# One level of Strassen's algorithm for the first feed-forward product, and the second product in three slabs

## The chip, the cores and the metric

The kernel runs on one core of a Trainium2 chip. The metric is the device time of one execution in microseconds (us); 3 runs of the kernel before gave a median of 3263.25 us (3255.14 to 3263.57).

## What is computed

Two transformer layers with adaptive norms, then one block of a second kind, all on 512 tokens of width 1024 in float32. The change touches the feed-forwards, of which there are six: two in each of the two layers, two in the last block. Cut to what matters:

```
D_MODEL, SEQ, D_FF, DEPTH = 1024, 512, 2816, 2

def swiglu(h, w13, w2):
    a, b = jnp.split(h @ w13, 2, axis=-1)
    return (jax.nn.silu(a) * b) @ w2

cond = jax.nn.silu(c)
for l in range(DEPTH):
    mod = (cond @ ada_w[l] + ada_b[l]).reshape(B, N_SUBLAYERS, 3, 1, D)
    h = adaln_pre(x, norm_g[l, 0], mod[:, 0, 0], mod[:, 0, 1])
    x = x + 0.5 * mod[:, 0, 2] * swiglu(h, ffn1_w13[l], ffn1_w2[l])
    h = adaln_pre(x, norm_g[l, 1], mod[:, 1, 0], mod[:, 1, 1])
    ...
    x = x + mod[:, 1, 2] * (y @ w_out[l])
    h = adaln_pre(x, norm_g[l, 2], mod[:, 2, 0], mod[:, 2, 1])
    x = x + 0.5 * mod[:, 2, 2] * swiglu(h, ffn2_w13[l], ffn2_w2[l])
```

adaln_pre is a row norm times (1 + scale) plus shift. The last block has the same kind of feed-forward with separate gate and up weights, a row norm ahead of it and one behind it.

## The kernel before

Activations lie transposed: the 1024 features as 8 blocks (KD) of 128 partitions, the 512 tokens as columns. Every float32 matmul operand is split in two reduced-precision parts, hi and lo, and a product of two such pairs is three matmuls (`mm3`, lines 306 to 315): hi x hi, hi x lo, lo x hi, all with the weights as the stationary 128 x 128 operand. The normed rows lie in `hh` and `hl`.

A weight tile comes in by `wchunk` (line 287): one DMA of 512 KB on SP's queue into one of four `raw` buffers, then for each half an ACT copy `hi` (line 296) and a DVE subtraction `lo` (line 297).

`ffn` (line 668) is the feed-forward. Its first product goes over NF = 22 column chunks j of 128: `products(j)` loads the gate chunk and the up chunk and runs for each 8 blocks k x 3 matmuls of 512 columns into one PSUM bank. The chunk before is finished meanwhile: ACT takes silu of the gate, DVE multiplies by up, POOL makes the pair `uh`, `ul` (lines 717 and 720); in the last block DVE multiplies both by the row norm first (713, 714). All 22 chunks of `uh` and `ul` stay in SBUF. The second product goes over the 8 output blocks d: 22 x 3 matmuls of 512 columns into one bank, then `emit_d` adds to `x` and collects squares for the next norm. The last d is run in two halves of 256 tokens, and `link` (line 639) uses that: while PE runs the second half, DVE, ACT and POOL norm the first half of the tokens (`prenorm` or `scaled`), and the next item's first products start on that half (`first`, `first_k`).

The modulation vectors `mod` come from a background generator (`mod_steps`, line 377): a step loads one 512 KB tile of `ada_w` into a `raw` buffer and adds it, scaled, to `acc` on DVE (lines 384, 386); after eight steps PE transposes and DVE reduces. Each call of `bg` (line 499) makes a step three times in four; `mod(l, s, r)` runs the generator on where a vector that is needed is not there:

```
    def mod(l, s, r):
        while (l, s, r) not in mods:
            next(bg_it)
        return mods[l, s, r]
```

`bg` is called after each gate or up chunk from j = 1 on and after each third of a d in the second product. The program is written in this order, and a scheduler of the framework then sets the order of each engine's instructions, within what buffers and data allow; on the chip every engine takes its own in that order.

## Time and profile before

| | us |
|---|---|
| median of 3 runs | 3263.25 |
| profiled execution | 3260.46 |
| its span, first to last instruction | 3258.7 |
| PE busy | 3184.6 (98%) |
| DVE busy | 1725.5 (53%) |
| ACT busy | 1211.0 (37%) |
| POOL busy | 744.1 (23%) |

The mean granted clock of PE is 0.990 of full speed. A busy share is an average over stages: a feed-forward's stages are found by the names of their tiles (`hh` and `hl` against `uh` and `ul`), and the wait that counts in one is the wait of PE. PE is matmuls, PEld the weight loads that overlap them.

### The profile page before, as it was taken

The numbers are of one execution on the slowest core, as the hardware profiler recorded it, in microseconds if no ns is written. First come the engines' busy times: TensorE is split into PE (matmuls) and PEld (weight loads), VectorE is DVE, ScalarE is ACT, GpSimd is POOL, SyncE is SP. The second block draws the span as 40 slices with busy tenths as digits, with TensorE's granted clock in tenths as the row PEclk, the third lists the DMA queues.
The fourth block names the chain that finished last, engine by engine and source line by source line (L and its number), as shares of the span: only waits on it lengthen the run. The fifth ranks groups of instructions, "written<-read, shape, count | busy, mean of one in ns | idle before, by whom it ended". The sixth has DMA issues, their size and how long they took to land.

```text
span 3258.7 us, 43061 instructions
## 1 busy us (share of the span) xinstructions
PE 3184.6 (98%) x16168; PEld 2676.0 (82%) x16168; DVE 1725.5 (53%) x2942; ACT 1211.0 (37%) x2287; POOL 744.1 (23%) x754
## 2 busy tenths in 40 slices
PE   7999999999999999999999999999999999999998
PEld 5888887888888888888888888888888888888887
DVE  6555576666555555536766633344443444664433
ACT  3222254553222232224555532233223355652232
POOL 3221222214221222212122322211221210231111
PEclk8999999999999999999999999999999999999999
DMA  6555642113555445543321234333323355442233
GB/s 232 186 165 169 193 136 78 40 60 132 164 172 164 155 149 168 165 124 119 106 63 37 104 103 137 120 117 104 128 101 95 125 179 146 132 135 97 96 93 105
DMA packets 135825, 414.98 MB, mean 127 GB/s; under 512 B 16777, under 2 KB 30221, under 8 KB 135345
## 3 DMA queue, kind: packets, MB, share of 16 engines
q1 hardware_dynamic: 129408, 391.27, 37.2%
q0 software_dynamic: 6064, 20.76, 2.1%
q8 instruction: 127, 2.08, 0.3%
q14 instruction: 82, 0.66, 0.1%
q10 hardware_dynamic: 144, 0.21, 0.0%
HBM read 379.58 MB, written 22.51 MB: 123 GB/s over the span
## 4 chain that ended last, share of the span: by engine, by line
PE 90%; DVE 4%; ACT 2%; POOL 2%; issue 1%; DMA 1%; SPq 0%; DVEq 0%; ACTq 0%; POOLq 0%
PE m L311 14%; PE m L312 14%; PE m L308 14%; PE a L308 11%; PE a L312 11%; PE a L311 11%; PE o L1408 2%; PE pt L1402 1%; DVE lo L297 1%; PE a L1176 1%; PE a L1192 1%; PE num L1354 1%; DVE t L621 0%; DVE hl L623 0%; PE hid L947 0%
## 5 line engine op out<-in xcount | busy, mean ns | idle before, releaser
L297 DVE TENSOR_TENSOR lo<-raw,hi 128x512 fp32r<-128x512 f32 (+2 forms) x1056 | 805.6, 768 | 942.9 <-ACT hi L296 916.4
L296 ACT CAST hi<-raw 128x512 fp32r<-128x512 f32 (+2 forms) x1056 | 639.2, 611 | 1637.3 <-PE m L311 891.5
L308 PE MATMUL m<-hh,hi 128*128 128x512 f32 (+1 forms) x1728 | 669.4, 387 | 13.6 <-ACT hh L474 7.4
L311 PE MATMUL m<-hl,hi 128*128 128x512 f32 (+1 forms) x1728 | 663.7, 384 | 5.3 <-DVE hl L633 2.2
L312 PE MATMUL m<-hh,lo 128*128 128x512 f32 (+1 forms) x1728 | 661.2, 383 | 1.6 <-DVE lo L297 1.6
L311 PE MATMUL a<-hl,hi 128*128 128x512 f32 (+1 forms) x1264 | 476.3, 377 | 1.0 <-DVE hl L623 1.0
L308 PE MATMUL a<-hh,hi 128*128 128x512 f32 (+1 forms) x1264 | 475.9, 376 | 0.0
L312 PE MATMUL a<-hh,lo 128*128 128x512 f32 (+1 forms) x1264 | 475.3, 376 | 0.0
L308 PEld LDWEIGHTS m<-hh,hi 128*128 128x128 f32 x1728 | 327.9, 190 | 76.8 <-ACT hh L474 7.6
L311 PEld LDWEIGHTS m<-hl,hi 128*128 128x128 f32 x1728 | 328.2, 190 | 67.3 <-DVE hl L633 3.7
L312 PEld LDWEIGHTS m<-hh,lo 128*128 128x128 f32 x1728 | 327.6, 190 | 64.8 <-DVE lo L297 6.3
L717 POOL TENSOR_SCALAR uh<-u 128x512 fp32r<-128x512 f32 x132 | 112.3, 851 | 1101.7 <-DVE u L710 692.8
L311 PEld LDWEIGHTS a<-hl,hi 128*128 128x128 f32 x1264 | 239.4, 189 | 44.5 <-DVE hl L623 1.8
L312 PEld LDWEIGHTS a<-hh,lo 128*128 128x128 f32 x1264 | 239.3, 189 | 43.9 <-DVE lo L297 1.1
L308 PEld LDWEIGHTS a<-hh,hi 128*128 128x128 f32 x1264 | 239.3, 189 | 42.9 <-ACT hi L296 0.5
L308 PE MATMUL a<-uh,hi 128*128 128x512 f32 (+1 forms) x660 | 229.7, 348 | 0.6
L311 PE MATMUL a<-ul,hi 128*128 128x512 f32 (+1 forms) x660 | 229.5, 348 | 0.0
L312 PE MATMUL a<-uh,lo 128*128 128x512 f32 (+1 forms) x660 | 228.7, 347 | 0.0
L308 PE MATMUL m<-uh,hi 128*128 128x512 f32 x528 | 205.8, 390 | 0.0
L720 POOL TENSOR_TENSOR ul<-u,uh 128x512 fp32r<-128x512 f32 x132 | 203.0, 1538 | 10.8
L312 PE MATMUL m<-uh,lo 128*128 128x512 f32 x528 | 205.4, 389 | 0.0
L311 PE MATMUL m<-ul,hi 128*128 128x512 f32 x528 | 205.4, 389 | 0.0
(462 smaller groups left out, 3965.6 us busy)
## 6 DMA issues: line engine op xcount, KB each, us to landing
raw<-in_ada_dram SPq DMA_DIRECT2D x144, 512.0 KB, 4.3
raw<-in_f1a_dram SPq DMA_DIRECT2D x88, 512.0 KB, 4.2
raw<-in_f2a_dram SPq DMA_DIRECT2D x88, 512.0 KB, 3.6
raw<-in_win_dram SPq DMA_DIRECT2D x48, 512.0 KB, 3.3
raw<-in_g1a_dram SPq DMA_DIRECT2D x44, 512.0 KB, 3.6
raw<-in_g2a_dram SPq DMA_DIRECT2D x44, 512.0 KB, 3.6
raw<-in_f1b_dram SPq DMA_DIRECT2D x32, 512.0 KB, 3.7
raw<-in_f2b_dram SPq DMA_DIRECT2D x32, 512.0 KB, 3.5
```

The lines of the kernel that those rows point to most:

```text
L296: order["hi"] = S.copy(h, raw[:, s])
L297: order["lo"] = V.tensor_tensor(l, raw[:, s], h.bitcast(F32), op=ALU.subtract)
L308: i = PE.matmul(o, wh, xh, start=start, stop=False)
L311: PE.matmul(o, wh, xl, start=False, stop=False)
L312: j = PE.matmul(o, wl, xh, start=False, stop=stop)
L717: G.tensor_scalar(uh[:, j], u, 1.0, 0.0, op0=ALU.mult, op1=ALU.add)
L720: order["ul"] = G.tensor_tensor(ul[:, j], u, uh[:, j].bitcast(F32), op=ALU.subtract)
L1176: PE.matmul(p[:, bs_], B[:, bs_], Z[:, bs_], start=True, stop=True)
L1192: PE.matmul(p[:, bs_], RT[:, bs_], w[:, bs_], start=True, stop=True)
L1354: PE.matmul(pn[:, i * 65:i * 65 + 65], wt[j][:, (i - j) * 128:(i - j) * 128 + 128], vd[:, j, h], start=j == 0, stop=j == i)
L1402: PE.transpose(pt[:, j * 128:j * 128 + 128], t[:, j * 128:j * 128 + 128], ident)
L1408: PE.matmul(o, r[:, j * 128:j * 128 + 128], v, start=j == 0, stop=j == len(vs) - 1)
```

## The change

The first product. Features are split in two halves (k 0 to 3, 4 to 7), tokens in two (0 to 255, 256 to 511), and the output in gate and up: a 2 x 2 x 2 block product, which one level of Strassen's algorithm (in Winograd's form) does in seven products instead of eight. Each product p of chunk n is 4 blocks x 3 matmuls of 256 columns. The class `Units` lists the products in order (p = 1, 2, 5, 6, then 4 of the chunk before, 3, 7) together with the second product's pieces, and `ahead` prepares each one's weights up to five units early: sums of weights on POOL and DVE, then `hi` and `lo` as before. `product` runs a product, several of them accumulating in bank A, which ACT copies out in between (`snap`); `after` builds gate and up from the copies.

The tokens. `block0` prepares the first half of the tokens as before, and keeps the plain rows in `hk`; `block1` makes the differences of the halves and their pairs (second half of `hh`, `hl`, and the new `eh`, `el`). `mod_first` does the same at the start, with seven load buffers instead of fourteen.

The second product runs in three slabs of 6, 8 and 8 chunks, after chunk 6, chunk 14 and chunk 21; the first two are added into `x` by `emit_d.acc`. Only the slab's `uh` and `ul` are kept. `bg` is called once per chunk and after two in three pieces of a slab. The bias rows `rows` move to the mixer and to POOL's queue, and the post norm's factor `gh` moves from the copy out of PSUM to the norm.

The core of the diff:

```diff
...
     def x_open():
...
+        xbox["eh"] = p.tile([128, 4, 3, 256], F32R, name=nm("eh"))
+        xbox["el"] = p.tile([128, 4, 3, 256], F32R, name=nm("el"))
+        xbox["hk"] = p.tile([128, KD, 256], F32, name=nm("hk"))
...
-                        raw = IN.tile([128, 1024], F32, tag="raw", bufs=14, name=nm("raw"))
+                        raw = IN.tile([128, 1024], F32, tag="raw", bufs=7, name=nm("raw"))
...
             def norm(k):
-                t = w_("t")
+                f = dict(scale=m[1][:, k:k + 1], bias=m[0][:, k:k + 1])
+                t = two(hk[:, 2 * k:2 * k + 2]) if k < 4 else w_("t")
                 vec(V.tensor_scalar(t, xr[:, k], m[1][:, k:k + 1], m[0][:, k:k + 1], op0=ALU.mult, op1=ALU.add))
+                if k < 4:
+                    dep(S.activation(hh[:, k, HV[0]], xr[:, k, HV[0]], AF.Identity, **f), order["hi"])
+                    vec(V.tensor_tensor(t1[k], t[:, HV[1]], t[:, HV[0]], op=ALU.subtract))
+                    S.copy(hh[:, k, HV[1]], t1[k])
+                    vec(V.tensor_tensor(hl[:, k, HV[0]], t[:, HV[0]], hh[:, k, HV[0]].bitcast(F32), op=ALU.subtract))
+                    vec(V.tensor_tensor(hl[:, k, HV[1]], t1[k], hh[:, k, HV[1]].bitcast(F32), op=ALU.subtract))
+                    return
...
+                t2 = IN.tile([128, 3, 256], F32, tag="t2", bufs=2, name=nm("t2"))
+                vec(V.tensor_tensor(t2[:, 0], t[:, HV[1]], t1[k], op=ALU.subtract))
+                G.tensor_tensor(t2[:, 1], t[:, HV[1]], hk[:, 2 * k + 1], op=ALU.subtract)
+                G.tensor_tensor(t2[:, 2], t[:, HV[0]], t2[:, 0], op=ALU.subtract)
+                S.copy(eh[:, k], t2)
+                vec(V.tensor_tensor(el[:, k], t2, eh[:, k].bitcast(F32), op=ALU.subtract))
...
+    def hl_of(dst, src, n=None):
+        h, l = (a if n is None else a[n] for a in dst)
+        run["cur"].append(S.copy(h, src))
+        V.tensor_tensor(l, src, h.bitcast(F32), op=ALU.subtract)
+
+    def block0(k, make, shift):
+        t = xbox["hk"][:, k]
+        make(t, k, HV[0])
+        h, l = hh[:, k, HV[0]], hl[:, k, HV[0]]
...
+            run["cur"].append(S.activation(h, t, AF.Identity, bias=shift[:, k:k + 1]))
+            V.scalar_tensor_tensor(l, t, shift[:, k:k + 1], h.bitcast(F32), op0=ALU.add, op1=ALU.subtract)
...
+    def block1(tt, shift):
...
+        for k in range(4):
+            q1.append(tmp("q1"))
+            sub(q1[k][:, h0], tt[k][:, h0], hk[:, k])
+            hl_of((hh[:, k, h1], hl[:, k, h1]), q1[k][:, h0])
+        for k in range(4):
+            sub(q1[k][:, h1], tt[k][:, h1], q1[k][:, h0], sh(k))
+            hl_of((eh[:, k, 0], el[:, k, 0]), q1[k][:, h1])
...
+        for k in range(4):
+            q2.append(tmp("q2"))
+            sub(q2[k][:, h0], tt[k][:, h1], tt[k][:, h0], None if shift is None else ds[:, k:k + 1])
+            sub(q2[k][:, h1], hk[:, k + 4], q1[k][:, h1], sh(k))
+            v = q2[k].rearrange("p (a b) -> p a b", a=2)
+            hl_of((eh[:, k, 1:3], el[:, k, 1:3]), v)
...
+    NU, NA = 18, 3
+    SLABS = (list(range(16, 22)), list(range(0, 8)), list(range(8, 16)))
+    JS = sum(SLABS, [])
+
+    class Units:
...
+            for n in range(n0, len(JS)):
+                u += P_(n, 1, 2, 5, 6) + P_(n - 1, 4) + P_(n, 3, 7)
+                if n in ends:
+                    u += self.down(ends[n])
+            u += P_(len(JS) - 1, 4) + self.down(2)
...
+        def load(self, i):
+            self.live = [r for r in self.live if self.last[r] >= i]
+            while self.loads and len(self.live) < 4 and self.first[self.loads[0]] < i + 10:
...
+        def ahead(self):
...
+                if p == 5:
+                    new(G, 1, half(b, 0), half(b, 1), ALU.add)
+                elif p == 6:
+                    new(V, 2, S_[1], half(a, 0), ALU.subtract)
+                elif p == 3:
+                    new(G, 4, half(a, 1), S_[2], ALU.subtract)
+                    new(G, 3, half(a, 0), half(b, 0), ALU.subtract)
...
+            h, l = self.tile(fp, "hi")[:, :w], self.tile(fp, "lo")[:, :w]
+            order["hi"] = S.copy(h, src)
+            order["lo"] = V.tensor_tensor(l, src, h.bitcast(F32), op=ALU.subtract)
+            self.q.append((h, l))
...
+        def take(self):
+            while len(self.q) < 5 and self.at < len(self.units) and (box.get("fp") or not self.q):
+                self.ahead()
...
+        def product(self):
...
+                for i, (w, x) in enumerate(((wh, xh), (wh, xl), (wl, xh))):
+                    PE.matmul(q, w[:, s], x, start=p in (1, 2, 5) and k + i == 0, stop=k == 3 and i == 2,
+                              skip_group_check=p not in (1, 2, 5))
+            return n, p
+
+        def after(self, n, p, done, norm):
...
+            def snap(q, b):
+                S_[q] = fp.tile([128, 256], F32, tag="sn", bufs=5, name=nm("sn"))
+                S.copy(S_[q], S_[b][:, 0:256])
+            if p == 1:
+                snap(1, "A")
+            elif p == 2:
+                S_["g"] = fp.tile([128, 512], F32, tag="ga", bufs=3, name=nm("ga"))
+                V.tensor_tensor(S_["g"][:, HV[0]], S_[1], S_["B"][:, 0:256], op=ALU.add)
+            elif p == 5:
+                snap(5, "D")
+            elif p == 6:
+                snap(2, "A")
+            elif p == 3:
+                g = S_["g"]
+                V.tensor_tensor(g[:, HV[1]], S_[2], S_["D"][:, 0:256], op=ALU.add)
+                if norm is not None:
+                    V.tensor_tensor(g, g, box["r"], op=ALU.mult)
+                act(g, g, AF.Silu)
+                if norm is not None:
+                    V.tensor_tensor(g, g, box["r"], op=ALU.mult)
+            elif p == 7:
+                snap(3, "A")
+                S_["c"] = fp.tile([128, 256], F32, tag="c", bufs=2, name=nm("c"))
+                G.tensor_tensor(S_["c"], S_[3], S_[5], op=ALU.add)
+            else:
+                u, g = w_("u"), S_["g"]
+                V.tensor_tensor(u[:, HV[0]], g[:, HV[0]], S_["A"][:, 0:256], op=ALU.mult)
+                V.tensor_tensor(u[:, HV[1]], g[:, HV[1]], S_["c"], op=ALU.mult)
+                uh, ul = (fp.tile([128, 512], F32R, tag="u", bufs=NU, name=nm("u")) for _ in range(2))
+                S.copy(uh, u)
+                order["ul"] = G.tensor_tensor(ul, u, uh.bitcast(F32), op=ALU.subtract)
...
+                f.after(n, p, u, norm)
+                if p == 4:
+                    if n > 2 and side is not None:
+                        next(side, None)
                     bg()
...
+                for d in range(KD if s < 2 else KD - 2):
+                    q = psa() if d % 2 else psm()
+                    for h in range(2):
+                        x, ws = f.take()
+                        assert x == ("D", s, d, h)
+                        mm(q, ws, us[h * m:h * m + m], ALL, h * m, 2 * m)
+                        if (2 * d + h) % 3:
+                            bg()
+                    if s < 2:
+                        emit_d.acc(d, q, s == 0)
+                    else:
+                        emit_d(d, q, ALL, False)
...
+        def acc(d, q, first):
+            xd = xbox["x"][:, d]
+            V.scalar_tensor_tensor(xd, q, g()[:, d:d + 1], xd, op0=ALU.mult, op1=ALU.add)
...
```

How it moves instructions, at three places.

DVE at the link from the first mixer to the second feed-forward, before (`t` is the scaled row block, `hl` its low part with the shift `mod_2915`, `lo` a weight split, line 790 adds the old product to `x`):

```order
L790 SCALAR_TENSOR_TENSOR x_6512<-a_6762,mod_2116,x_6512 128x256
L621 SCALAR_TENSOR_TENSOR t_6903<-x_6512,mod_2541,r_6589 128x256
L621 SCALAR_TENSOR_TENSOR t_6907<-x_6512,mod_2541,r_6589 128x256
L297 TENSOR_TENSOR lo_6892<-raw_6889,hi_6891 128x512
L623 SCALAR_TENSOR_TENSOR hl<-t_6903,mod_2915,hh 128x256
L623 SCALAR_TENSOR_TENSOR hl<-t_6907,mod_2915,hh 128x256
```

and now (`hk` in place of `t`, `mod_8548` the same shift, `acc_8523` its sum, `ds` a difference of shifts):

```order
L711 SCALAR_TENSOR_TENSOR hk_8138<-x_8135,mod_4590,r_8215 128x256 x5
...
L895 TENSOR_TENSOR lo_8634<-raw_8507,hi_8633 128x512
L895 TENSOR_TENSOR lo_8646<-raw_8509,hi_8645 128x512
L386 TENSOR_SCALAR acc_8523<-raw_8524,cond 128x1024
L388 SCALAR_TENSOR_TENSOR acc_8523<-raw_8527,cond,acc_8523 128x1024
...
L388 SCALAR_TENSOR_TENSOR acc_8523<-raw_8545,cond,acc_8523 128x1024
L397 TENSOR_REDUCE mod_8548<-a_8549 128x4
L397 TENSOR_REDUCE mod_8548<-a_8555 128x4
L398 TENSOR_TENSOR mod_8548<-mod_8548,cols 128x8
L674 TENSOR_TENSOR ds_8750<-mod_8548 128x4
L663 SCALAR_TENSOR_TENSOR hl<-hk_8138,mod_8548,hh 128x256 x8
L895 TENSOR_TENSOR lo_8652<-S_8649,hi_8651 128x512
```

Between the scaled rows and their low parts there now stand the eight steps of a modulation vector and its reductions; before, that vector's steps stood inside the first feed-forward.

SP's DMA issues at the same link, now (`raw_8505` to `raw_8511` are the first weights of the second feed-forward, the `in_ada` loads belong to the eight steps; in the built program the first of these and all behind it have the address of `raw_8505`):

```order
L848 DMA raw_8505<-in_f2a_dram 128x1024
L848 DMA raw_8507<-in_f2a_dram 128x1024
L848 DMA raw_8509<-in_f2a_dram 128x1024
L848 DMA raw_8511<-in_f2a_dram 128x1024
L384 DMA raw_8524<-in_ada_dram 128x1024
L384 DMA raw_8527<-in_ada_dram 128x1024
...
L384 DMA raw_8545<-in_ada_dram 128x1024
L848 DMA raw_8808<-in_f2a_dram 128x1024
```

The weights take all four `raw` buffers ahead of the eight loads, and the next weights stand behind these.

DVE over one chunk in the middle of a first product, now (`S` a sum of weights, `ga` the gate, `sn` a copy out of PSUM, `A`, `B`, `D` the banks, `c` a sum on POOL):

```order
L895 TENSOR_TENSOR lo_3402<-raw_3132,hi_3401 128x512
L895 TENSOR_TENSOR lo_3427<-S_3422,hi_3426 128x512
L960 TENSOR_TENSOR u_3500<-ga_3292,c_3399 128x256
L895 TENSOR_TENSOR lo_3446<-S_3424,hi_3445 128x512
L940 TENSOR_TENSOR ga_3443<-sn_3418,B_3430 128x256
L895 TENSOR_TENSOR lo_3467<-raw_3313,hi_3466 128x512
L881 TENSOR_TENSOR S_3527<-S_3507,raw_3313 128x512
L895 TENSOR_TENSOR lo_3485<-raw_3313,hi_3484 128x512
L895 TENSOR_TENSOR lo_3510<-S_3507,hi_3509 128x512
L959 TENSOR_TENSOR u_3500<-ga_3292,A_3254 128x256
L895 TENSOR_TENSOR lo_3530<-S_3527,hi_3529 128x512
L947 TENSOR_TENSOR ga_3443<-sn_3482,D_3449 128x256
```

A chunk had four `lo` and one multiplication here; it has seven `lo`, one sum and four operations of 256 columns.

## Rows read from the trace of the kernel before

**Rows 1.** The page: its first line, busy time of each engine, the chain that ended last.

```profile
span 3258.7 us, 43061 instructions
...
PE 3184.6 (98%) x16168; PEld 2676.0 (82%) x16168; DVE 1725.5 (53%) x2942; ACT 1211.0 (37%) x2287; POOL 744.1 (23%) x754
...
PE 90%; DVE 4%; ACT 2%; POOL 2%; issue 1%; DMA 1%; SPq 0%; DVEq 0%; ACTq 0%; POOLq 0%
```

**Rows 2.** Timeline of PE: start us, duration us, instruction; 512 columns, then 256.

```profile
238.92 0.39 PE L308 MATMUL m<-hh,hi 128*128 128x512 f32 x1
...
243.00 0.39 PE L308 MATMUL m<-hh,hi 128*128 128x512 f32 x1
...
413.77 0.28 PE L312 MATMUL a<-uh,lo 128*128 128x256 f32 x1
...
417.73 0.28 PE L312 MATMUL a<-uh,lo 128*128 128x256 f32 x1
```

**Rows 3.** Groups of DVE: line, form, count | busy us, mean ns | idle before, releaser.

```profile
L623 DVE SCALAR_TENSOR_TENSOR hl<-t,mod,hh 128x256 fp32r<-128x256 f32 x80 | 37.6, 513 | 2.4 <-ACT hh L622 2.4
...
L1180 DVE TENSOR_TENSOR w<-a,lvl 128x256 f32<-128x256 f32 x56 | 22.7, 421 | 13.4 <-PE a L1176 13.1
...
L790 DVE SCALAR_TENSOR_TENSOR x<-a,mod,x 128x256 f32<-128x256 f32 x12 | 5.8, 479 | 27.8 <-PE a L312 27.8
...
L476 DVE TENSOR_TENSOR hl<-t,hh 128x512 fp32r<-128x512 f32 x8 | 6.4, 806 | 1.1 <-ACT hh L474 0.6
...
L473 DVE TENSOR_SCALAR t<-xr,mod,mod 128x512 f32<-128x512 f32 x8 | 5.3, 665 | 0.2
```

**Rows 4.** One line's instructions, L386 on DVE: ns min/median/max, first and last start.

```profile
L386 DVE SCALAR_TENSOR_TENSOR acc<-raw,cond,acc x112: 1271/1281/2319, 63.6 to 1388.4; 128x1024 f32<-128x1024 f32 x112
```

**Rows 5.** Groups of ACT and of POOL, columns as in rows 3.

```profile
L296 ACT CAST hi<-raw 128x512 fp32r<-128x512 f32 x944 | 582.1, 622 | 1464.6 <-PE m L311 804.7 <-PE a L311 593.9 <-PE a L1653 23.3
...
L720 POOL TENSOR_TENSOR ul<-u,uh 128x512 fp32r<-128x512 f32 x132 | 203.0, 1538 | 10.8
...
L619 POOL TENSOR_TENSOR t<-t,r 128x256 f32<-128x256 f32 x30 | 25.3, 845 | 34.6 <-ACT r L259 32.9
```

**Rows 6.** Timelines of DVE and of POOL, 325 to 330 us, columns as in rows 2.

```profile
325.00 0.68 DVE L297 TENSOR_TENSOR lo<-raw,hi 128x512 fp32r<-128x512 f32 x1
325.60 2.06 DVE L386 SCALAR_TENSOR_TENSOR acc<-raw,cond,acc 128x1024 f32<-128x1024 f32 x1
327.59 1.64 DVE L297 TENSOR_TENSOR lo<-raw,hi 128x384 fp32r<-128x384 f32 x1
...
325.17 1.42 POOL L580 TENSOR_TENSOR sq<-x 128x512 f32<-128x512 f32 x1 [13.54 <-DVE x L790]
326.66 2.15 POOL L588 TENSOR_TENSOR st<-st,sq 128x512 f32<-128x512 f32 x1
```

**Rows 7.** The same timelines near 1850 us.

```profile
1849.81 0.48 DVE L790 SCALAR_TENSOR_TENSOR x<-m,mod,x 128x256 f32<-128x256 f32 x1 [1.52 <-PE m L312]
...
1849.26 1.29 POOL L588 TENSOR_TENSOR st<-st,sq 128x512 f32<-128x512 f32 x1
```

**Rows 8.** DMA issues: tile and source, count, KB each, median us to landing.

```profile
raw<-in_ada_dram SPq DMA_DIRECT2D x144, 512.0 KB, 4.3
...
raw<-in_f2a_dram SPq DMA_DIRECT2D x88, 512.0 KB, 3.6
```

**Rows 9.** Timeline of PE at a link, with idle time before and its releaser in brackets.

```profile
1142.73 0.70 PE L586 MATMUL st<-sq,ones 128*128 128x256 f32 x2 [1.95 <-ACT sq L582]
...
1144.44 0.41 PE L311 MATMUL m<-hl,hi 128*128 128x256 f32 x1
1144.65 0.41 PE L312 MATMUL m<-hh,lo 128*128 128x256 f32 x1
```

**Rows 10.** Windows: us, busy us of PE, PEld, DVE, ACT, POOL, then granted clock, DMA.

```profile
44.00:48.00 4.00, 1.86 (x8) 1.78 (x8) 3.89 (x4) 0.00 (x0) 1.80 (x2) 0.57 0.00 0
1144.00:1146.00 2.00, 2.00 (x11) 2.00 (x11) 1.57 (x3) 1.09 (x3) 0.96 (x1) 0.50 0.00 0
```

More of the change, by code (lines that the diff above doesn't have):

```diff
@@ L488, in mod_first @@
             load(4)
-            first_k(cs, q0, ALL, range(4))
+            for _ in range(4):
+                f.product()
             scale(4)
@@ L626, in scaled, with times, make @@
+    def times(gain):
+        def make(t, k, sl):
+            i = S.activation(t, xbox["x"][:, k, sl], AF.Copy, scale=gain[:, k:k + 1])
+            run["cur"].append(i)
+        return make
     def scaled(k, gain, sl):
```

349 lines of the change are left out of this document (258 added, 91 removed).

## The prediction

> **What bounds the kernel now.** I read the page first: TensorE (PE) is busy 98% of the span and holds 90% of the chain that ended last, VectorE (DVE) is at 53%, ScalarE (ACT) at 37%, GpSimd (POOL) at 23% [rows 1]. The reader should see that only fewer or shorter PE instructions save time, and that the cover is thinnest on DVE. The timeline of PE gives the price: a matmul's listed 0.39 or 0.28 us has a modelled end, its start-to-start time counts. 512 columns: 18 starts in 4.08 us, 0.2267 us each. 256 columns: 33 starts in 3.96 us, 0.120 us each [rows 2]; at neither width does the weight load show. Then the groups of DVE, ACT and POOL and two timelines of DVE beside POOL [rows 3 to 7] say what the added work costs, the DMA issues what a late load costs [rows 8], a link and two windows what an idle PE costs [rows 9, 10].
>
> **The gain on PE.** One column chunk j of the first product was 48 matmuls of 512 columns, 48 x 0.2267 = 10.88 us; it becomes seven products of 12 matmuls of 256, 84 x 0.120 = 10.08 us. 0.80 us x 22 chunks x 6 feed-forwards = 106 us. Chunk 0 of five feed-forwards was run in halves (96 x 0.120 = 11.52), 0.64 us more each: 3 us. The second product goes from 462 long and 132 short matmuls to 480 and 96, 120.6 to 120.3 us: 1.5 us in all. Together **-110 us**. It is earned only where PE never waits; five things take from it.
>
> **DVE and POOL per chunk.** By the new order a chunk takes, on DVE, seven splits `lo` and one sum of 512 columns and four operations of 256; on POOL four of 512 (three sums and `ul`) and one of 256; on ACT thirteen, about 7 us at 0.62 for a long one [rows 5], within 10.08. On DVE one instruction follows another after 0.60 us (512 columns) [rows 6], 1.20 (1,024: 1.28 less the 0.08 that neighbours overlap) [rows 4] and 0.34 (256: 0.42 less 0.08) [rows 3]: 8 x 0.60 + 4 x 0.34 = 6.2 us, which fits. But in rows 6 DVE needs 4.23 us for a split, a 1,024 step and a 384-wide split, which alone take 0.60 + 1.20 + 0.56 (the last put between 0.42 and 0.69): the two POOL operations beside them cost DVE 1.87 us, 0.93 each. Operations with two SBUF inputs take turns with POOL's. One that reads PSUM does not: 0.48 us in the middle of a POOL instruction [rows 7], its group's mean [rows 3]. So a chunk needs 6.2 + 4 x 0.93 + 0.45, less 0.3 of the 1.0 us of PSUM reads that I let run beside POOL: 10.1 us. Where modulation steps are interleaved (0.75 of 1.20 + 0.2 for reductions per chunk, the first three feed-forwards) it is 11.1; where the row norm multiplies twice more (the last two) 11.3. Against PE's 10.08 that is a new bound, by little. Weights are prepared five products ahead, 7.2 us of PE time, and the slabs of the second product, light on DVE, refill that lead before chunks 7 and 15; the first stretch of seven starts without it, behind the link. Loss with steps: 7 x 1.05, then 8 x 1.05 - 7.2, then 0.2, in all 8.8, three times; with the norm 8.5 + 2.6 + 1.3, twice. **+51 us**. Ends: 0, if POOL falls where DVE waits anyway, and 266, if each POOL operation costs DVE all of its 1.29 us [rows 7] and nothing runs beside it (1.7 us more per chunk). I take 0.93: it was measured with both queues full, as they will be.
>
> The Trainium skill, SBUF — State Buffer, section "Who interferes with whom", says that a DVE instruction with two SBUF inputs and a GpSimd instruction that reads SBUF shut each other out for the whole instruction. This case's trace agrees that they take turns, but at 0.93 of 1.29 us; what the full length would make of the time is rival 2.
>
> **The link into a feed-forward (five times).** Before, PE idles 1.95 us there for one square on ACT [rows 9]. Now the second half of the tokens needs differences of halves. From the end of the old product to the last `el` the order has on DVE 55 operations of 256 columns (0.34, or 0.43 with a scalar [rows 3]; 0.37 on average), 20 us, and 13 of 512, 8 us; on POOL 12 of 256 (half their 0.85 us [rows 5] each) and 5 of 512, 10 us more: 38 us, some 7 of it before that end or beside PSUM reads. PE has nine products, 13 us, up to product 7 of chunk 0, which needs that last `el` and which the order puts ahead of the other chunks' fifth products. So about 18 us idle for 2: I take +15, +12 at the two links where ACT makes the scaled rows, and +8 at the one where the next item lets DVE and POOL run ahead. **+62 us**; ends 25 (POOL off the path and two thirds of DVE's work covered) and 100.
>
> **A load that is now late.** The modulation vectors come from a background generator: three in four calls of `bg` make a step, eight steps a vector. A feed-forward had 63 calls, 48 steps, six vectors; it has 50 now, and with three forced steps five vectors. The sixth, the shift of the second feed-forward, is forced inside its link: on DVE its eight steps stand between the `hk` rows and their `hl`, on PE its transposes ahead of the first product. Three of the four `raw` buffers hold weights, so the built program sends its eight 512 KB loads through the one that `raw_8505` leaves, each behind the step before it. A landing takes 3.6 us (weights) to 4.3 (this tensor's median, under load) [rows 8], a step 1.28 [rows 4]: 8 x (3.6 + 1.28 + 0.3, my choice for the signals) = 41, with 5 until the buffer is free, 2.5 for transposes and reductions, less 4 that the link idles anyway: **+45 us**. Ends: 14 (one landing, then the steps back to back) and 57. Two smaller ones: in feed-forwards 1 and 2 three or four steps are forced ahead of the first slab's first sum; the lead of five units of 2.0 us covers most: **+10**, ends 0 and 25.
>
> **Start, clock, the rest.** The start hangs on DVE (3.89 of 4 us busy at a PE that is half idle [rows 10]). Preparing a row group there took 0.67 + 0.81 us [rows 3]; four now take 0.67 + 3 x 0.42, four 0.67 + 0.81 + 0.42 + 0.95 (768 columns): +7.3 us, and half as many load buffers may add some: **+8**, ends 0 and 15. After the idle at the link the granted clock is 0.50, the 1.2 GHz level, for two us, with short matmuls 0.21 us apart [rows 9, 10]; one more such stretch per link: **+5**, ends 0 and 30. The slabs' sums into `x` (16 per feed-forward, each at most two of the 0.48 us of 256 columns [rows 3]) cost nothing beside matmuls of over 4 us each; without that cover, at most 92. The bias rows' load moves from SP's to POOL's queue at a mixer's head: 0.
>
> Sum: -110 + 51 + 62 + 45 + 10 + 8 + 5 = +71 on the profiled execution's 3260.5 us, which is 2.8 below the median of 3263.25: **3331 us**, 2% slower. A measurement of this kernel can tell about 0.3%, 10 us, from no change.
>
> **Rivals.** (1) DVE keeps PE's pace, and the change is faster. If a POOL operation costs DVE under some 0.7 us, a chunk stays near 10.08 even with a step, the stretches lose nothing and the links 25: -110 + 0 + 25 + 40 + 5 + 5 + 0 = -35, 3226 us. For it: POOL could slip into DVE's waits for ACT. Against it: rows 6. Chance 0.20. (2) POOL's operations cost DVE their full length: 215 more than my sum, 3546 us. For it: a 384-wide split that lasts 1.64 us; against it: the total of the same rows 6. 0.07. (3) The late load is spread over several buffers after all: 31 less, 3300 us. Against it: the one buffer. 0.08. (4) The change does not shorten PE: above 0.1295 us a short matmul eats the gain. Against it: 33 in a row at 0.120. I leave it inside the forecast's case.
>
> **The numbers.** The forecast's case has 0.65: 0.62 slower, 0.03 within 0.3%. Rival 1 is faster, 0.20; rival 3 slower 0.05, same 0.03; rival 2 slower 0.07. So faster 0.20, same 0.06, slower 0.74. The range of 3240 to 3430 leaves out rival 2 and half of rival 1; inside it several costs stand at one of their ends together.
>
> **What would show it.** Right: first-product matmuls 0.120 us apart; PE idle time released by `lo` and `el` on DVE; one stretch of some 45 us without matmuls near 760 us, with eight loads of `in_ada` in turn; splits well over 0.69 us on average; slices at half clock behind the links. Wrong: DVE with idle time throughout the first product, or no such hole; and if PE waits mostly for ACT's copies out of PSUM, the bound is one that I did not price.

## The result and the profile after

The changed kernel takes **3622.83 us** (median of 4 runs, 3619.22 to 3626.09), the kernel before 3261.72 us beside it: a ratio of **1.1111, 95% interval 1.109 to 1.1132**. It is slower, as forecast, but by 361 us where the forecast said 71, and far outside the range. The profiled execution spans 3623.4 us. The page, and the granted clock of the core (span, mean clock), answer to [rows 1]:

```profile
span 3623.4 us, 55479 instructions
...
PE 3222.2 (89%) x20572; PEld 2893.4 (80%) x20572; DVE 2536.2 (70%) x4109; ACT 1669.4 (46%) x3431; POOL 1343.2 (37%) x1162
...
PEclk6999999997999999999999999999999999979999
```

```profile
core 0: 3623.4 us, clock 0.949
```

No engine is as full as PE was; every engine waits for another. The clock stood at 0.990 before: the half-clock time, (1 - clock) x 2 x span, went from 65 to 370 us. The waits of PE (what waited, for which instruction: us in total, times, longest us) name the places:

```profile
PE A L925 <- ACT sn L935: 116.8, 92, 4.3
PE a L396 <- DVE acc L388: 101.2, 15, 44.6
PE D L925 <- ACT hh L651: 15.6, 4, 4.5
PE D L925 <- DVE lo L895: 14.7, 16, 2.3
PE A L925 <- DVE lo L895: 12.7, 25, 3.1
PE B L925 <- DVE hl L489: 11.1, 4, 3.7
PE A L925 <- ACT eh L651: 10.2, 11, 4.6
PE A L925 <- ACT hh L651: 10.2, 1, 10.2
```

The first line is new: products 6, 7 and 4 add to a bank whose sum `sn` ACT must have copied out. The second is a vector's transposes behind the vector's last sum. The `hh`, `eh`, `hl` lines are the links and the start. The waits are counted between modelled ends; below I count from starts instead. I took every start-to-start time of PE, took off what its width costs at full clock [rows 2], put up to a half-clock matmul's extra down to the clock while the granted clock was 0.50 (256 columns then start 0.213 us apart), and the rest to the instruction that ended the wait:

```
us                                   before     after
widths at full clock                   2955      2845    -110
half clock                               19        98     +79
waits over 0.3 us                        74       435    +361
  of these, for sn                        0       131
  for acc, one hole / 14 others           0    45 + 58
  for lo                                  3        44
smaller differences                     211       245     +34
```

PE's matmuls, counted at the prices of [rows 2], come to 110 us less, as forecast; 474 us were lost against it. Where: windows over the second stretch of the first product (eight chunks, between the first two slabs; the third stretch is the rest, up to the last slab) of feed-forward 2, which runs modulation steps, and of feed-forward 5, which runs none. Columns: us, then busy us and instructions of PE, PEld, DVE, ACT, POOL, then granted clock, DMA share, GB/s.

```profile
1040.20:1148.00 107.80, 89.89 (x680) 86.76 (x679) 78.15 (x107) 48.10 (x102) 46.99 (x36) 0.94 0.37 122
2638.30:2728.00 89.70, 83.21 (x673) 82.20 (x672) 85.02 (x106) 49.67 (x102) 53.67 (x43) 0.98 0.34 112
```

PE alone needs 8 x 10.08 = 81 us. Feed-forward 5 takes 11.2 us a chunk with DVE 95% busy: there DVE is the bound. Feed-forward 2 takes 13.5 us a chunk, and DVE is busy only 72% of it. The groups of DVE say why, first for feed-forward 2 (busy us, mean ns | idle before, releaser), then for 5:

```profile
L895 DVE TENSOR_TENSOR lo<-S,hi 128x512 fp32r<-128x512 f32 x31 | 31.2, 1007 | 0.0
L895 DVE TENSOR_TENSOR lo<-raw,hi 128x512 fp32r<-128x512 f32 x26 | 21.6, 842 | 1.9 <-ACT hi L894 1.8
L388 DVE SCALAR_TENSOR_TENSOR acc<-raw,cond,acc 128x1024 f32<-128x1024 f32 x6 | 8.2, 1374 | 12.5 <-DMA raw<-in_ada_dram 12.5
L881 DVE TENSOR_TENSOR S<-S,raw 128x512 f32<-128x512 f32 x7 | 5.9, 836 | 13.1 <-POOL S L881 13.1
...
L940 DVE TENSOR_TENSOR ga<-sn,B 128x256 f32<-128x256 f32 x8 | 3.3, 410 | 0.0
```

```profile
L895 DVE TENSOR_TENSOR lo<-S,hi 128x512 fp32r<-128x512 f32 x30 | 31.5, 1059 | 2.1 <-ACT hi L894 1.9
L895 DVE TENSOR_TENSOR lo<-raw,hi 128x512 fp32r<-128x512 f32 x26 | 25.7, 1016 | 0.0
L949 DVE TENSOR_TENSOR ga<-ga,r 128x512 f32<-128x512 f32 x7 | 10.4, 1492 | 0.1
```

A split of 0.69 us lasts a full microsecond beside POOL; a sum that reads PSUM (L940) does not lengthen. And in feed-forward 2, six steps keep DVE standing 12.5 us for their loads, and seven sums S2 stand 13.1 us for POOL's S1, which waits in its turn (group of POOL, same stretch) for weights whose loads share the four buffers with the steps':

```profile
L881 POOL TENSOR_TENSOR S<-raw 128x512 f32<-128x512 f32 x7 | 9.4, 1337 | 32.9 <-DMA raw<-in_f2a_dram 32.9
```

How a late DVE reaches PE is seen in the timelines of DVE, ACT and PE of feed-forward 6 (start us, us, instruction [idle before, releaser]):

```profile
3403.26 0.41 DVE L947 TENSOR_TENSOR ga<-sn,D 128x256 f32<-128x256 f32 x1
3403.70 1.61 DVE L949 TENSOR_TENSOR ga<-ga,r 128x512 f32<-128x512 f32 x1
...
3407.08 1.20 DVE L881 TENSOR_TENSOR S<-S,raw 128x512 f32<-128x512 f32 x1 [1.16 <-POOL S L881]
```

```profile
3405.35 0.63 ACT L259 ACTIVATE ga<-ga 128x512 f32<-128x512 f32 x1 [1.44 <-DVE ga L949]
3405.88 0.35 ACT L935 COPY sn<-A 128x256 f32<-128x256 f32 x1
3406.14 1.14 ACT L894 CAST hi<-S 128x512 fp32r<-128x512 f32 x2
3407.18 0.37 ACT L935 COPY sn<-A 128x256 f32<-128x256 f32 x1
```

```profile
3407.60 0.39 PE L925 MATMUL A<-eh,hi 128*128 128x256 f32 x1 [1.67 <-ACT sn L935]
```

One gate multiplication takes 1.61 us for 0.69; ACT's Silu waits for it; two copies and two roundings stand behind the Silu in ACT's queue; PE waits for the second copy, while DVE has the weights of this product and the next ready (counted from the feed-forward's start, 104 low parts finished and 102 products and slab pieces begun). DVE itself stands 1.16 us for POOL's sum.

This does not begin with the stretch. Its first three chunks run at PE's pace, 10.1, 10.1 and 10.3 us; the five others take 11.9 to 12.1 us each. The windows over these three, over four of the others, and DVE's group with idle time in the second window:

```profile
3346.90:3377.40 30.50, 30.50 (x254) 30.30 (x253) 26.89 (x34) 17.63 (x36) 16.54 (x12) 1.00 0.25 87
3383.60:3431.60 48.00, 41.32 (x336) 40.50 (x336) 43.67 (x58) 24.65 (x53) 25.54 (x20) 1.00 0.26 87
```

```profile
L881 DVE TENSOR_TENSOR S<-S,raw 128x512 f32<-128x512 f32 x4 | 4.8, 1198 | 4.6 <-POOL S L881 4.6
```

A late chunk is 10.9 us of DVE's time and 1.2 us in which DVE stands for POOL.

### The profile page after: what moved, and what is told of

Its sections match the earlier page's. It is cut to its first block, busy times and chain, and to the rows that moved or that the text cites. A ratio compares the mean times of both kernels' runs of the same rounds, so it can differ in the third digit from the quotient of the medians.

```text
span 3623.4 us, 55479 instructions
## 1 busy us (share of the span) xinstructions
PE 3222.2 (89%) x20572; PEld 2893.4 (80%) x20572; DVE 2536.2 (70%) x4109; ACT 1669.4 (46%) x3431; POOL 1343.2 (37%) x1162
## 5 line engine op out<-in xcount | busy, mean ns | idle before, releaser
L895 DVE TENSOR_TENSOR lo<-raw,hi 128x512 fp32r<-128x512 f32 (+1 forms) x684 | 586.4, 872 | 122.3 <-ACT hi L894 118.9
L894 ACT CAST hi<-raw 128x512 fp32r<-128x512 f32 (+1 forms) x684 | 405.4, 606 | 515.2 <-PE a L311 222.3
L925 PE MATMUL A<-eh,hi 128*128 128x256 f32 x1584 | 475.9, 300 | 133.0 <-ACT sn L935 116.8
L895 DVE TENSOR_TENSOR lo<-S,hi 128x512 fp32r<-128x512 f32 x528 | 521.0, 996 | 43.6 <-ACT hi L894 41.7
L894 ACT CAST hi<-S 128x512 fp32r<-128x512 f32 x528 | 323.0, 618 | 415.0 <-POOL S L881 223.8
L925 PE MATMUL A<-eh,lo 128*128 128x256 f32 x1584 | 465.6, 294 | 11.8 <-DVE lo L895 11.2
L925 PE MATMUL A<-el,hi 128*128 128x256 f32 x1584 | 464.8, 293 | 8.0 <-DVE el L652 8.0
L297 DVE TENSOR_TENSOR lo<-raw,hi 128x512 fp32r<-128x512 f32 (+1 forms) x240 | 176.7, 747 | 129.6 <-ACT hi L296 121.0
L308 PE MATMUL m<-hh,hi 128*128 128x512 f32 (+1 forms) x632 | 248.6, 393 | 4.4 <-ACT d_k L1192 2.6
L311 PE MATMUL m<-hl,hi 128*128 128x512 f32 (+1 forms) x632 | 244.0, 386 | 6.2 <-DVE hl L734 3.4
L312 PE MATMUL m<-hh,lo 128*128 128x512 f32 (+1 forms) x632 | 242.3, 383 | 5.0 <-DVE lo L297 5.0
L296 ACT CAST hi<-raw 128x512 fp32r<-128x512 f32 (+1 forms) x240 | 143.8, 613 | 213.3 <-PE m L311 134.5
```

Of the source, the lines that this page charges most:

```text
L296: order["hi"] = S.copy(h, raw[:, s])
L297: order["lo"] = V.tensor_tensor(l, raw[:, s], h.bitcast(F32), op=ALU.subtract)
L308: i = PE.matmul(o, wh, xh, start=start, stop=False)
L311: PE.matmul(o, wh, xl, start=False, stop=False)
L312: j = PE.matmul(o, wl, xh, start=False, stop=stop)
L894: order["hi"] = S.copy(h, src)
```

## The experiments

Times are medians; each run stands beside its own runs of the kernel before. Theory A, formed from the lines above: POOL's operations and late loads hold DVE's queue, and PE follows DVE through the copies.

**The steps called more often.** Undoes one part of the change: the calls of `bg`.

```
-                        if (2 * d + h) % 3:
-                            bg()
+                        bg()
```

> Every unit of a slab now calls the background generator, where one unit in three did not: 66 calls in a feed-forward for 50. In the changed kernel TensorE stood still 103 us in 15 places behind a forced modulation step, 44.7 of them in the one hole near 850 us. Theory A (the vectors come late because the calls became fewer): the hole and most of the other 14 waits go, the released time is 80 to 100 us, about 3530 to 3550 us, and the waits for the PSUM copies (131 us) stay or grow by some 10, because VectorE gets more steps earlier. Theory B (VectorE is full, so a step costs TensorE the same wherever it stands): the hole goes but comes back as waits for the PSUM copies, at most 20 us faster, 3600 to 3625 us.

Measured: 3607.24 us, ratio 1.1048 (1.1016 to 1.108), some 16 us faster. The hole of 45 us is gone. But the last matmul of the first feed-forward, which now makes six vectors, came at 520.3 us for 498.6, and the other waits for `acc` grew from 58 to 74 us. Theory B had the size right, with the wait in another place than it said. Moved into the feed-forward, the steps of this vector cost PE most of what they had cost at the link.

**All sums on VectorE.** The five POOL operations of a chunk move; the code is otherwise the same.

```
-                    new(G, 1, half(b, 0), half(b, 1), ALU.add)
+                    new(V, 1, half(b, 0), half(b, 1), ALU.add)
...
-                    new(G, 4, half(a, 1), S_[2], ALU.subtract)
-                    new(G, 3, half(a, 0), half(b, 0), ALU.subtract)
+                    new(V, 4, half(a, 1), S_[2], ALU.subtract)
+                    new(V, 3, half(a, 0), half(b, 0), ALU.subtract)
...
-                G.tensor_tensor(S_["c"], S_[3], S_[5], op=ALU.add)
+                V.tensor_tensor(S_["c"], S_[3], S_[5], op=ALU.add)
...
-                order["ul"] = G.tensor_tensor(ul, u, uh.bitcast(F32), op=ALU.subtract)
+                order["ul"] = V.tensor_tensor(ul, u, uh.bitcast(F32), op=ALU.subtract)
```

> The three sums of weight halves, the low part of u and the sum c move from GpSimd to VectorE; nothing else changes. Theory A (a GpSimd operation costs VectorE about 0.93 us of turns, more than the 0.60 it would take there itself, and TensorE waits through the PSUM copies for a VectorE that is behind): VectorE needs 12 x 0.60 + 5 x 0.34 = 8.9 us a chunk, under the 10.08 of TensorE; the waits for PSUM copies fall from 131 us to some 30, those for splits from 38 to some 15, the half-clock time by half: 3440 to 3490 us. Theory B (VectorE is the bound by its own work): 2.7 us more a chunk, 130 chunks, up to 3700 us or more. Theory C (the weights' loads come late, the engines do not matter): 3600 to 3640 us, GpSimd's 480 us of waiting for loads turn up on VectorE.

Measured: 3410.82 us, ratio 1.0446 (1.0416 to 1.0476): **212 us faster**, more than expected. The line of busy times, the window over the second stretch of feed-forward 5, and two groups of DVE in it:

```profile
PE 3150.1 (92%) x20572; PEld 2847.7 (84%) x20572; DVE 2515.4 (74%) x4769; ACT 1688.9 (50%) x3431; POOL 427.6 (13%) x502
```

```profile
2479.30:2559.80 80.50, 80.50 (x673) 80.50 (x672) 77.14 (x142) 51.86 (x103) 0.00 (x0) 1.00 0.34 106
```

```profile
L895 DVE TENSOR_TENSOR lo<-S,hi 128x512 fp32r<-128x512 f32 x30 | 20.4, 686 | 2.3 <-ACT hi L894 2.1
...
L963 DVE TENSOR_TENSOR u<-u,u 128x512 fp32r<-128x512 f32 x8 | 5.5, 685 | 0.1
```

DVE took 660 operations more and was busy 21 us less. The chunk is at PE's own pace, at full clock. The 35 operations that came over in this stretch cost DVE 28 x 0.60 + 7 x 0.34 = 19.2 us; without them it had 57.9 us of work, and in the changed kernel 85.0. So POOL's operations there (27 of 512 columns, 7 of 256) cost DVE 27.1 us, 0.89 us per 512 columns. That is the fullest stretch. The same sum over the other second and third stretches gives 0.5 to 0.6 us in feed-forwards 1 to 3, where DVE is idle a quarter of the time, and 0.7 to 0.85 in 4 to 6; over the whole run, 0.64. Waits for `sn` fell from 131 to 20 us, for the `lo` of L895 from 38 to 5. The edit takes away the turns, and with them DVE's and ACT's waits for POOL's sums; it does not tell the two apart.

**Both edits.** The two diffs above together.

> Both edits together: sums on VectorE and a call of the generator in every slab unit. Theory A: the two gains add, because one is a wait for the late steps and the other a VectorE that is behind: 3623 - 90 - 160, 3340 to 3400 us. If the steps' gain was only room on VectorE that the other edit also gives: 3430 to 3490 us, no better than the sums alone.

Measured: 3394.03 us, ratio 1.0395 (1.0365 to 1.0425). It lies in Theory A's range, but because the sums gave more; the steps gave 17 us, as alone.

**A buffer of its own for the steps' loads.** In `mod_steps`, inside a feed-forward:

```
+            fp = box.get("fp")
-            raw = WB.tile([128, 1024], F32, tag="raw", bufs=4, name=nm("raw"))
+            raw = (WB.tile([128, 1024], F32, tag="raw", bufs=4, name=nm("raw")) if fp is None else
+                   fp.tile([128, 1024], F32, tag="ada", bufs=1, name=nm("ada")))
```

> Inside a feed-forward the modulation steps' loads get one buffer of their own instead of taking turns in the weights' ring of four. Theory C (the ring is the bound: VectorE sat idle 184 us before modulation steps waiting for their loads, GpSimd 480 us before its sums waiting for weights): the first four feed-forwards gain 15 to 25 us each, 3530 to 3570 us. Theory A (VectorE's turns with GpSimd are the bound; its waits for loads are partly slack): 3590 to 3620 us. The hole near 850 us stays in both, as it lies where the buffer of its own does not exist yet.

Measured: 3549.53 us, ratio 1.0871 (1.0839 to 1.0903), 73 us faster, as Theory C said, which yet explains no more than that: feed-forwards 5 and 6 are as long as they were. With POOL's sums where they were, DVE stood 93 us for steps' loads instead of 184. Loads that hold DVE's queue are a second cost beside POOL's turns.

**Only the low part of `u` to VectorE.**

```
-                order["ul"] = G.tensor_tensor(ul, u, uh.bitcast(F32), op=ALU.subtract)
+                order["ul"] = V.tensor_tensor(ul, u, uh.bitcast(F32), op=ALU.subtract)
```

> Of the five GpSimd operations of a chunk only the low part of u goes to VectorE; no TensorE instruction is near it, it is read by the next slab. Theory A, turns (a GpSimd operation holds VectorE up by about 0.93 us, wherever its result goes): VectorE gains 0.93 - 0.60 = 0.33 us in each of 132 chunks, 44 us, and as TensorE follows a late VectorE, 3560 to 3600 us. Theory D, chain (what the sums cost is the way GpSimd, VectorE, GpSimd, ScalarE that each weight sum goes through, not the turns): the low part is on no such way, VectorE gets 80 us more work, 3620 to 3690 us.

Measured: 3614.01 us, ratio 1.1089 (1.1019 to 1.1159). Neither range: 9 us faster by the medians, 19 by the profiled spans. DVE's busy time rose by 15 us (2536.2 to 2550.9) for 132 operations that alone take 79, so this POOL operation had cost DVE about 0.48 us, where all five together come to 0.64. Its two runs lie 15 us apart, so that it is faster is not shown, and the run settles nothing.

**The sums issued two units earlier.** A method `make(j)` holds the sums of unit j, once for each unit and only if both its weights are already under way; preparing unit i calls it for the next two units.

```
+                self.make(i, fp, half)
+                for j in range(i + 1, min(i + 1 + 2, len(self.units))):
+                    if fp is not None:
+                        self.make(j, fp, half)
```

> GpSimd keeps its sums, but each is issued two units earlier than the rounding that reads it. In the changed kernel ScalarE waited 224 us for GpSimd's sums with the PSUM copies behind it in its queue, VectorE 138 us. Theory D, chain: these two waits fall under 80 and 50 us, the waits for PSUM copies from 131 to under 50, 3500 to 3550 us. Theory A, turns: the same operations beside each other cost the same, the waits change their names, 3590 to 3630 us.

Measured: 3625.51 us, ratio 1.1124 (1.108 to 1.1169). Inconclusive: the waits that the edit was meant to remove hardly moved (ACT 224 to 212 us, DVE 138 to 136), and POOL itself still stood 463 us for the loads of feed-forwards 1 to 4 (482 before the edit): where the weights are not there, a sum cannot be issued earlier.

**More room behind the copies.** The order of products.

```
-                u += P_(n, 1, 2, 5, 6) + P_(n - 1, 4) + P_(n, 3, 7)
+                u += P_(n, 1, 2) + (P_(n - 1, 7) if n > n0 else []) + P_(n, 5, 6) + P_(n - 1, 4) + P_(n, 3)
...
```

> Product 7 of a chunk moves behind products 1 and 2 of the next, so that product 6 has three products (4.3 us) behind the copy of the sum it adds to where it had two (2.9), and product 7 four where it had two. Theory E, slack (TensorE waits because a bank of PSUM is copied out and added to again within 2.9 us): the waits for PSUM copies fall from 131 to under 50 us, 3510 to 3560 us. Theory A (VectorE needs more than a chunk's 10.08 us, any slack is used up after two chunks): at most 40 us less, 3580 to 3625 us, with longer waits for splits in their place.

Measured: 3634.34 us, ratio 1.1151 (1.1106 to 1.1197). Waits for `sn` 113 us instead of 131, for `lo` 48 instead of 38, for `acc` 112 instead of 103. The copies are where the lateness shows, not its cause: Theory E falls. The time also lies 9 us above Theory A's range.

**A candidate.** The first two edits, the buffer for the loads, and:

```
-            if k < KD - 1:
-                yield
+            yield
...
-        if bgn[0] % 4:
-            next(bg_it, None)
+        next(bg_it, None)
```

> Sums on VectorE, as before; the generator called in every slab unit and without leaving out every fourth call; a modulation step's load in a buffer of its own within a feed-forward; a vector's transposes one step behind its last sum, so that TensorE does not meet them while VectorE still waits for the last load. With both earlier edits 3394 us, 51 us of it waits for the last sum of a vector in 13 places. If these waits are only there because transposes stand right behind the sum: they go under 10 us, 3310 to 3350 us. If VectorE is still behind at these places: 3360 to 3395 us.

Measured: 3388.27 us, ratio 1.0396 (1.0354 to 1.0439): the second case. Waits for `acc` became fewer and longer, 9 with 61 us, the longest 17, in the slabs, where calls come 2 us apart and the one buffer serves a load only each 3.5.

**Work on POOL that nobody waits for.** To the kernel with all sums on VectorE:

```
+                scr = fp.tile([128, 512], F32, tag="scr", bufs=1, name=nm("scr"))
+                for _ in range(4):
+                    G.tensor_tensor(scr, uh.bitcast(F32), ul.bitcast(F32), op=ALU.add)
```

> The kernel with all sums on VectorE (3411 us) gets four GpSimd additions of 512 columns per chunk whose result nobody reads: as many as it took away, but no engine waits for them. Theory A, turns: VectorE is held up by them as by the sums before, four times some 0.93 us a chunk; it is 96% busy at 10.05 us a chunk in the last two feed-forwards, which become 12.5 to 13.5 us a chunk, the first four some 2 us a chunk longer: 3600 to 3750 us. Theory D, chain (the loss was the way of each weight sum through three engines): nothing waits for these additions, 3410 to 3430 us.

Measured: 3853.25 us, ratio 1.1814 (1.178 to 1.1848), 442 us more than without these additions. The stretch of feed-forward 5, its splits, and the additions on POOL:

```profile
2784.50:2892.60 108.10, 88.19 (x674) 86.12 (x673) 105.37 (x140) 49.62 (x103) 48.77 (x37) 0.94 0.30 95
```

```profile
L895 DVE TENSOR_TENSOR lo<-raw,hi 128x512 fp32r<-128x512 f32 x25 | 25.6, 1027 | 0.5 <-ACT hi L894 0.5
```

```profile
L966 POOL TENSOR_TENSOR scr<-u,u 128x512 f32<-128x512 f32 x28 | 43.9, 1567 | 78.4 <-DVE u L963 76.8
```

DVE does the same work and is busy 105.4 us for 77.1: 28.2 us for 28 additions, **1.0 us each**. The timelines show the turns: beside four additions in a row DVE's operations start 1.67 us apart, where they start 0.60 apart without them.

```profile
2808.49 6.31 POOL L966 TENSOR_TENSOR scr<-u,u 128x512 f32<-128x512 f32 x4 [7.68 <-DVE u L963]
```

```profile
2808.58 1.73 DVE L895 TENSOR_TENSOR lo<-raw,hi 128x512 fp32r<-128x512 f32 x1
2810.24 1.74 DVE L949 TENSOR_TENSOR ga<-ga,r 128x512 f32<-128x512 f32 x1
2811.91 1.75 DVE L895 TENSOR_TENSOR lo<-S,hi 128x512 fp32r<-128x512 f32 x1
...
2815.61 0.68 DVE L895 TENSOR_TENSOR lo<-S,hi 128x512 fp32r<-128x512 f32 x1
```

This shows that turns alone cost so much: no result of these additions is used, no engine waits for one, and DVE is 97% busy. That the chain costs nothing in the changed kernel is not shown by it; DVE's 1.2 us a chunk for POOL's sum, above, are of the chain. Theory A's upper end was still too low, 3750.

**No modulation steps.** This kernel leaves out a part of the computation. The 128 steps (the text on record counts the 112 of one line) give way to:

```
+        V.tensor_copy(m, C(("adab", l), (3 * s + r) * 8, 8))
```

> The changed kernel with its sums on GpSimd as they are, but the modulation vectors after the first two are not computed: each is only its bias, so 112 steps, their loads and their transposes are left out. Theory F (a step costs far more than its 1.28 us, since VectorE's queue stands still until its load has landed, 184 us in all, and TensorE stands behind the transposes, 103 us): the second and third stretches of the first three feed-forwards fall from 12.2 to 13.5 us a chunk to the 10.7 to 11.3 of the last three, the hole goes: 3420 to 3470 us. Theory G (a step costs VectorE its own time, the rest of the waits are slack): only the 103 us of forced waits and some 40 us go, 3480 to 3530 us.

Measured: 3398.68 us, ratio 1.042 (1.039 to 1.045), 224 us faster. The second stretch of feed-forward 2:

```profile
920.00:1005.00 85.00, 82.94 (x674) 81.07 (x673) 72.46 (x95) 49.56 (x104) 42.60 (x35) 1.00 0.31 100
```

10.6 us a chunk where it was 13.5, at full clock, with POOL's sums in place. 224 us are 1.75 us of PE's time per step; Theory F holds, and by 21 us more than its range. What is left is POOL's: the first four chunks take 10.1 us each, the others 10.7 to 11.3, and DVE stands 10.3 us for POOL's sums.

**A better candidate.** All sums on VectorE, own buffer, the next load issued as soon as a step is done, transposes one call later, every call a step, three slab units in four:

```
+            nxt = get(k + 1) if k < KD - 1 and box.get("pre") and box.get("fp") else None
             yield
...
```

> All sums on VectorE; a step's load goes to a buffer of its own and is issued when the step before it is done, not in the same call; the transposes one call later; every call of the generator makes a step, three slab units in four call it. The candidate before (3388 us) still had 61 us of waits for forced sums, and its calls stood close together in the slabs, 2 us apart, where a load takes 3.5. If the steps' cost is waiting for loads: the first three feed-forwards come near 10.3 to 10.8 us a chunk, the forced waits under 20 us, 3310 to 3350 us. If the steps' own VectorE time is the cost: 3370 to 3400 us.

Measured: 3358.53 us, ratio 1.0297 (1.0267 to 1.0327). The best version that computes everything, and between its two cases: forced waits 40 us, feed-forwards 1 to 3 at 11.8 to 13.0 us a chunk in the second stretch and 10.3 to 10.9 in the third. It does not beat the kernel before.

**Neither POOL's sums nor steps.** All sums on VectorE and no modulation steps, together; the same part of the computation is left out.

> Both at once: all sums on VectorE (alone 212 us faster than the changed kernel) and no modulation steps after the first two vectors (alone 224 us faster; the same part of the computation is left out as there). What stays of the change is TensorE's gain of 110 us, the links, the start and the half-clock stretches behind them. Theory H (one VectorE queue that is behind: what either edit frees is partly the same time): TensorE is the bound in the first product, 10.1 to 10.4 us a chunk in all second and third stretches; -110 + 61 (links) + 23 (start) + some 30 (clock) + 10 to 20 on the kernel before gives 3270 to 3300 us. Theory I (two separate losses that add): 3623 - 212 - 224, 3170 to 3200 us.

Measured: 3260.34 us, ratio 1.0 (0.9988 to 1.0011). Feed-forwards 2 and 5:

```profile
890.50:971.20 80.70, 80.70 (x674) 80.70 (x673) 71.05 (x129) 52.23 (x103) 0.00 (x0) 1.00 0.34 106
2329.10:2409.80 80.70, 80.70 (x674) 80.67 (x673) 77.21 (x142) 52.02 (x103) 0.00 (x0) 1.00 0.34 106
```

PE is the bound in every second stretch but that of feed-forward 4. The gains of the two edits, 212 and 224, come to 363 together: 73 us were lost to both at once, as Theory H has it for one queue, though 10 us under its range. What is left of the change gives and takes the same. Counted as above, this run has 119 us less than the kernel before at PE's widths (9 of them transposes that it leaves out), 90 us more of waits, nearly all at the links and the start, 22 more at half clock and 8 of smaller differences. The kernel before without its steps was not run.

## Why the prediction was wrong, step by step

The right sign came from the right mechanisms; four terms of the sum were too small. In the table the measured +207 is what the other lines leave of 364.

```
us                              forecast   measured
gain on PE                          -110       -110
DVE and POOL per chunk               +51       +207
links                                +62        +61
the late vector                      +45        +45
other forced steps                   +10        +58
start                                 +8        +23
half clock                            +5        +79
```

**Gain on PE: right.** 2955 to 2845 us, short matmuls 0.120 us apart.

**Links: right in sum, not in place.** PE's waits from the end of the old product to product 14, less those of before, are 8, 10, 8 and 8 us at the first four and 26 at the last, the one behind the last mixer. I had put +15 twice, +12 twice and +8, so that the sum came out is luck.

**The late vector: right.** One wait of 44.6 us at 851 us, with eight loads issued one behind the other on SP (first start, time to the end of the last), a landing of some 3.3 us and steps of 1.28:

```profile
896.22 1.97 PE L396 MATMUL a<-km,acc 128*128 128x128 f32 x8 [44.63 <-DVE acc L388]
```

```profile
858.92 32.68 SPq L384 DMA_DIRECT2D raw<-in_ada_dram  x8
```

But what I drew from it was wrong: I took the vector as the price of the missing calls, and calling more often gave back only 16 us.

**DVE and POOL per chunk: turns were right in kind, and three things were not.** The forecast took 0.93 us of DVE per POOL operation [rows 6]; the runs give 0.89 in the fullest stretch, 0.5 to 0.85 in the others and 1.0 with unused additions. The first failed step is the need of a chunk, 11.3 us with the row norm. The 11.2 to 11.5 us of the second and third stretches of feed-forwards 5 and 6 only look like it: they are averages with the first three chunks, which the lead carries at 10.1 to 10.3 us. A late chunk takes 12.0 us in feed-forward 6: 10.9 of DVE's time, less than the forecast, and 1.2 in which DVE stands for POOL's first sum, a wait that the forecast put at nothing. The step behind it, "the slabs of the second product, light on DVE, refill that lead", held: when the second stretch of feed-forward 6 begins, five weights are ready. With 12.0 in place of 11.3 the forecast's own sum, 8 x 1.92 - 7.2, gives 8.2 us lost; feed-forwards 5 and 6 lost 9 to 10 us in each second and third stretch, where I had 2.6 and 1.3. The rest is that the lead is not used up. It is one of weights; DVE's queue also carries the gate, in order among the splits, ACT's Silu waits for the gate, and behind the Silu stand the copies that PE's next product needs, so a late DVE stops PE with two weights in hand. The timelines above show the path, and more room behind the copies did not help.

The second failed step is 11.1 us for a chunk with steps: it took 12.2 to 13.5, and DVE was idle a quarter of the time. I had priced a step at its 1.20 us; its load is issued in the same call, through buffers that the weights fill, and DVE's queue stands till it has landed, 184 us in all. In the kernel before DVE never stood for such a load (the last column is idle time):

```profile
L386 DVE SCALAR_TENSOR_TENSOR acc<-raw,cond,acc 128x1024 f32<-128x1024 f32 x112 | 164.1, 1465 | 0.0
```

Third, where steps run, POOL's sums wait for weights, 32.9 us in the stretch of feed-forward 2 shown above. All second and third stretches together took 1104 us, 185 over 15.2 chunks x 6 x 10.08 (half clock and forced steps in them included); I had forecast 12.

**Other forced steps:** 58 us in 14 waits. "The lead of five units covers most" failed: the transposes stand in PE's queue and wait for the vector's last sum, whatever weights are ready. With the hole it was so for 15 of the 16 vectors, not only where steps are forced.

**Start:** between 59 and 72 us PE waits three times 3.4 to 3.9 us for the split `hl` of one more row, since DVE makes a row's difference and its low part of 768 columns ahead of the next row's `hl` and stands 1.7 us between the two for ACT's rounding of POOL's differences, and then 4.7 us for a weight's rounding. I had counted DVE's extra work, 7.3 us, and not that PE would wait for it row by row.

**Half clock:** "one more such stretch per link" failed. The trace has 52 stretches at 0.50, where the kernel before has 10; 163 us of them lie in the first stretches of the feed-forwards, 78 in the second and third, 44 more in the hole. Not every wait brings one. Of PE's waits in the first product that began at full clock, 10 of the 43 of one to two microseconds were followed by 0.50 within 2 us, and 13 of the 17 of 2.9 us and more; the waits of 1.7 us in feed-forward 6 shown above, one in 12 us, by none. Where the waits went, the clock came back: 1.00 in the second and third stretches of feed-forwards 4 to 6 without POOL's sums, 0.922 over the run with unused additions.

**Rivals.** Rival 1 fell: in feed-forwards 1 to 3 the price was under its 0.7 us, and DVE did not keep pace even so, since it stood for loads and sums. Rival 2 came nearest in time, 3546, for a wrong reason: its full length would make 13 us a chunk in feed-forwards 5 and 6, where a late chunk took about 12. Of the three signs against me that I named, two were there: DVE idle in the first product where steps run, and PE waiting mostly for ACT's copies. The copies are not the bound, but they were the sign that a lead of weights is not enough.

**The range.** Its ends took each cost by itself. The lengthened DVE operations and the late loads feed one another: the gains of the two edits overlap by 73 us. That the half clock does so too is not shown. All four misses went the same way.

## What to carry to other kernels

Before side work moves to an idle engine, price it on the engine that it takes turns with: here a sum on GpSimd cost VectorE some 0.9 to 1.0 us where VectorE was full, and on VectorE itself 0.60. Price also the waits along the way of a sum that passes through several engines, here 1.2 us a chunk. A lead puts a bound off and no more: five weights carried three chunks, and PE stood with two of them left, since something else that it needed was in the same queue. And a background step that issues its load in the same call can cost its queue the landing: nothing in the kernel before, 184 us here, where the loads share buffers with the weights.

## What the runs showed of the hardware

VectorE did 660 operations more in 21 us less busy time once GpSimd's were gone. The Trainium skill, SBUF — State Buffer, section "Who interferes with whom", has a VectorE instruction with two SBUF inputs contend with a GpSimd instruction that reads SBUF, under an exclusive lock; that this lasts for the whole instruction, as the prediction has it, stands in the page's section "SBUF: two separate sides". The runs agree: an addition that lasts 1.57 us on GpSimd costs VectorE 1.0 us (the 1.57 holds GpSimd's own turns of waiting: the shortest of the 528 lasted 1.26), and sums that read PSUM kept their 0.41 us (410 ns beside GpSimd, 413 without). The half-clock time, at the 1.2 GHz level, went from 65 to 370 us, in 52 stretches for 10; waits of one to two microseconds brought it in one case out of four, and five of them 12 us apart in no case.
